# Moving the steps of a hybrid decoder layer's small work between the big products: five places in the order, and one scaling from VectorE to ScalarE

## The chip, the cores and the metric

The kernel runs on one core of a Trainium2 chip. Its time is the device time of one execution in microseconds, as the median of several runs. A core has a matrix engine (TensorE, PE in the profile), a vector engine (VectorE, DVE), a scalar engine (ScalarE, ACT), GpSimd (POOL) and a queue engine (SP) that issues transfers. Each engine takes its instructions in the order in which they were written; between engines there are semaphores.

## What is computed

One layer over 256 tokens of 2048 features, all in float32: RMS norm, one input projection into everything that four token mixers need (queries, keys, values, two kinds of gates), four attention mixers, a projection of each, a gated sum, an output projection and a final norm.

```python
h = rms_norm(x, norm_w)
p = h @ w_in                       # z, gate, qkv of four mixers, indexer, forget gate
o_dsa  = dsa_attention(...)        # 16 index heads score keys, the top 64 are kept
o_fox  = forgetting_attention(...)
o_diff = differential_attention(...)   # two softmax maps, then an RMS norm per head
o_dil  = dilated_attention(...)
for b in range(4):
    y = branches[b] * silu(z_parts[b])
    term = sigmoid(g_parts[b]) * (y @ w_branch[b])
    merged = term if merged is None else merged + term
return rms_norm(x + merged @ w_out, final_norm_w)
```

## The kernel before

**Products.** A float32 product is made of three matmuls: the weights are split into a high part (whi, ScalarE, L193) and a residue (wlo, VectorE, L206), the activations likewise, and L362, L363 and L364 multiply high by high, high by low and low by high. The work is a list of *units*, each one weight tile of 1 MB in two halves; weights arrive by SP's queue in six slots (raw), and a slot is loaded again when its last reader has been issued. whi has a ring of 8 halves, wlo a ring of 6 (HI and LO). In the main loop (L1201 ff.) each half of unit i first issues the residue five halves ahead and the high part seven halves ahead, then the matmuls of its own.

**Strassen steps.** The projections of 2048 by 1024 columns are done by `seven`: block products (c2 and c1, each in two units of 24 matmuls, and the plain P1, P2 and P4) and forms in which sums of weight blocks multiply sums of activations (P3, P5, P6, P7). `plus` (L173, tile raw) adds one weight block to another on VectorE; sf is the sum of activations, split like the others (L428 ScalarE, L429 VectorE). Units P1 to P7 have 12 matmuls and `cost` 12, the c units 24. The order of the eleven units is the list returned at the end of `seven`: one for the projections of the branches, one (`late`) for the output.

**Threads.** All small work (attention, the indexer, norms, merging) is written as Python generators. After each unit its cost is added to `since`; when it reaches PACE, 20, every active thread is advanced to its next `yield`, and only then is a unit's own `start` list made active (`begin`). So where a thread's small products stand among TensorE's big ones, and where its VectorE and ScalarE work stands in their queues, is decided by the `yield` count and by the costs. The threads that matter here:
- `rms_thread`: 1/rms of the tokens as a row (rp on TensorE, rrow), ahead of branch 0; next to it the misc thread turns the indexer's and gate's columns (msT, mtp, fl, fe, lf, then the cumulative sums cps) and the bias tables (vps).
- The index thread of branch 0: ps_ix on TensorE, rel on ScalarE, sc on VectorE (L735, L737), then four steps of top-k (L745, L746: MAX and MATCH_REPLACE).
- The attention heads: logits (lps), exponential (lg), the division by the sum (`scaled`, L795), transposes (ptp), o, the gated result y and its two halves yT. In the diff branch od, a norm (`on`), and otd, its transpose.
- `merge_thread(n)`: adds the merged gates (L908, g), turns them (mtp, L916) into mT with its residue (L921). The output's products read mT.

In the threads one ring of four PSUM tiles (`att_ps`) serves all small products.

```python
since += u.cost
if since >= PACE:
    since = 0
    run_threads()
begin(u)
```

Of the kernel before, what the change touches and what calls it, by code (L numbers as in the profile page):

```python
# [81 lines left out]
class Unit:  # L82
# [5 lines left out]
    def __init__(self, raw, mm, post=(), need=(), start=(), pre=(), frees=None, loads=None):  # L88
        self.raw, self.k0, self.nk, self.n = raw, raw.k0, raw.nk, raw.n
        self.mm, self.post = mm, list(post)  # L90
        self.need, self.start, self.pre = list(need), list(start), list(pre)
        self.after = []
        self.frees = [raw] if frees is None else list(frees)
        self.loads = [raw] if loads is None else list(loads)
        self.parts = [[None, None], [None, None]]
        self.cost = 24

    def hi(self, k):
# [11 lines left out]
def body(ctx: ExitStack, tc, x, norm_w, w_in, fox_b_f, lq1, lk1, lq2, lk2, subln_w,  # L110
# [166 lines left out]
    def rms_thread():  # L277
# [9 lines left out]
        for t in range(2):  # L287
            nc.gpsimd.tensor_scalar(dg[:, t * P:(t + 1) * P], ident, rst[:, t:t + 1], None,
                                    op0=ALU.mult)
        yield  # L290
        yield
# [140 lines left out]
    def seven(src, c1, c2, base, ev, name, need={}, start=(), late=False):  # L432
# [47 lines left out]
        def unit(what, raw, mm, post=(), frees=(), loads=(), pre=()):  # L480
# [8 lines left out]
        u3 = unit("P3", B22, product("Z", form(0, 4), not late))  # L489
        u6 = unit("P6", B12, product("Y", form(0, 0)), [read(ev.u2, "Y")],  # L490
                  pre=[lambda: plus(B12, B22), lambda: free([B22])])
        u7 = unit("P7", B11, product("Y", form(1, 0)), [read(ev.u3, "Y")], frees=[B11],
                  pre=[lambda: plus(B11, B12, ALU.subtract)])
        u2 = unit("P2", B21, product("X", whole(0, s0 + 4), True))
        u2.after += [lambda: plus(B21, B12)] + ([] if late else [lambda: free([B12])])
        u4 = unit("P4", B21, product("Y", whole(1, s0 + 4)), frees=[B21])
# [6 lines left out]
        if late:  # L503
            u6.after += [lambda: free([B12])]
            u7.post += [read(ev.c12, "Z", True), read(ev.c22, "W", True)]
            return [c2a, c2b, u1, u5, u3, u2, u6, u7, c1a, u4, c1b]
        c2b.post += [read(ev.c12, "Z", True)]
# [285 lines left out]
    def scaled(e, r):  # L793
        for t in range(2):
            nc.vector.tensor_scalar(e[:, SL[t]], e[:, SL[t]], r[:, t:t + 1], None, op0=ALU.mult)  # L795

# [38 lines left out]
    def diff_thread(b, h):  # L835
# [40 lines left out]
        yield  # L876
        yield
        ot = att_ps("otd")
        for t in range(2):
# [22 lines left out]
    def merge_thread(n):  # L902
# [6 lines left out]
        if n < 2:  # L909
            load_m(n + 2)  # L910
        yield
        for i2 in range(2):
            tp = att_ps("mtp2")
# [14 lines left out]
    def branch_units(b, n):  # L928
        def ev(ps):
# [6 lines left out]
            elif n == 0:  # L936
                for i in range(2):
                    load_m(i)
        return tok_units(w_branch[b], n * 512, lambda k: (V["yT"][:, k, 0], V["yT"][:, k, 1]),
                         (0, 2, 4, 5)[n:n + 1], ev,  # L940
                         "ps_b", need=[f"att{b}"] if n == 0 else [],
                         start=[(f"merge{n}", lambda: merge_thread(n))] if b == 3 else [])


# [140 lines left out]
    for b, off, scale, fn in ((0, O_DSA, HSCALE, head_thread), (1, O_FOX, HSCALE, head_thread),  # L1085
                              (2, O_DIFF, 0.125, diff_thread), (3, O_DIL, HSCALE, head_thread)):
        units += qkvz_units(b, off, scale, att_threads(b, fn))
        for i in range(2):
# [107 lines left out]
    for i in range(RAMP, len(units)):  # L1196
        u = units[i]
        while any(a[0] in u.need for a in active):
            run_threads(u.need)
        for h in range(2):  # L1200
            low(2 * i + h + LO - 1)  # L1201
            high(2 * i + h + HI - 1)
            u.mm(u, h)
        for f in u.post:
            f()
        since += u.cost
        if since >= PACE:
            since = 0
            run_threads()
        begin(u)  # L1210
    while active:
# [27 lines left out]
```

## Time and profile before

| | |
|---|---|
| median of 3 runs | 1010.71 us (1009.23 to 1011.93) |
| the profiled execution | 1009.36 us |
| its span in the trace | 1007.7 us |
| TensorE (PE) busy | 958.3 us, 95% |
| VectorE (DVE) busy | 856.1 us, 85% |
| ScalarE (ACT) busy | 630.1 us, 63% |
| GpSimd (POOL) busy | 47.5 us, 5% |

The span is the time from the first to the last instruction that the trace shows. Engines overlap, so their busy times don't add up. A busy share is an average over the stages: the norm and the indexer's products to about 61 us, then four branches of about 209 us each (two `seven` products for q, k, z, v, two for the gates, four branch products), then the output from about 896 us.

### The profile page before, as it was taken

The page shows a single profiled execution, that of the slowest core. Times are in us where ns is not written, and L with a number is a line of the kernel's source. Part 1 is how long each engine was busy: PE and PEld are TensorE (multiplying, and loading weights), DVE is VectorE, ACT ScalarE, POOL GpSimd, SP SyncE. Part 2 cuts the span into 40 slices and gives each one's busy share as a digit, 9 for nine tenths or more (in the row PEclk, how much of TensorE's full clock was granted, in tenths as well). Part 3 has the DMA queues.
Part 4 walks back from the last instruction along what each step waited for, and adds up shares of the span by engine and source line. Part 5 has one row for each costly group of instructions (what it writes and reads, how often), then busy time and mean ns, then how long its engine had stood idle before and what let it go on. Part 6 is the DMA issues. An engine that isn't in the chain of part 4 may idle for free.

```text
span 1007.7 us, 12090 instructions
## 1 busy us (share of the span) xinstructions
PE 958.3 (95%) x4443; PEld 793.4 (79%) x4443; DVE 856.1 (85%) x1016; ACT 630.1 (63%) x809; POOL 47.5 (5%) x67
## 2 busy tenths in 40 slices
PE   9979996999999999999999999979999999985996
PEld 8857885778888888888888877868888888873786
DVE  5689999999898989987997998968898998499762
ACT  5756853697655667974566778745556796353541
POOL 2010000000000000000100000101000000100130
PEclk9999999899999999999999999989999999987999
DMA  9926463455767556468857464648755645931702
GB/s 319 295 90 222 139 212 122 168 167 204 264 220 238 180 170 235 173 201 260 233 173 246 170 202 132 213 164 207 257 182 173 220 174 201 392 135 42 264 29 84
DMA packets 100043, 195.81 MB, mean 194 GB/s; under 512 B 7811, under 2 KB 10021, under 8 KB 99600
## 3 DMA queue, kind: packets, MB, share of 16 engines
q1 hardware_dynamic: 96240, 181.06, 52.8%
q0 software_dynamic: 3712, 13.98, 5.3%
q8 instruction: 35, 0.57, 0.2%
q14 instruction: 24, 0.20, 0.1%
q10 hardware_dynamic: 32, 0.01, 0.0%
HBM read 186.61 MB, written 8.41 MB: 194 GB/s over the span
## 4 chain that ended last, share of the span: by engine, by line
PE 81%; DVE 10%; issue 3%; ACT 3%; DMA 2%; POOL 0%; ACTq 0%; POOLq 0%; DVEq 0%
PE ps_g L362 10%; PE ps_g L363 10%; PE ps_g L364 10%; PE ps_zv L362 5%; PE ps_zv L364 5%; PE ps_zv L363 5%; PE ps_qk L364 5%; PE ps_qk L362 5%; PE ps_qk L363 5%; DVE wlo L206 4%; PE ps_o L363 2%; PE ps_b L362 2%; PE ps_b L363 2%; PE ps_b L364 2%; PE ps_o L362 2%
## 5 line engine op out<-in xcount | busy, mean ns | idle before, releaser
L193 ACT ACTIVATE whi<-raw 128x1024 fp32r<-128x1024 f32 (+1 forms) x439 | 444.6, 1051 | 231.2 <-DVE raw L173 93.3
L206 DVE TENSOR_TENSOR wlo<-raw,whi 128x1024 fp32r<-128x1024 f32 (+1 forms) x439 | 519.0, 1218 | 52.5 <-ACT whi L193 19.1
L173 DVE TENSOR_TENSOR raw<-raw 128x2048 f32<-128x2048 f32 x68 | 155.6, 2288 | 30.8 <-DMA raw<-in_w_in_dram 30.2
L364 PE MATMUL ps_g<-wlo,hT 128*128 128x512 f32 x352 | 137.7, 391 | 8.3 <-DVE wlo L206 8.3
L362 PE MATMUL ps_g<-whi,hT 128*128 128x512 f32 x352 | 138.9, 395 | 1.4 <-ACT g L530 1.4
L363 PE MATMUL ps_g<-whi,hT 128*128 128x512 f32 x352 | 137.3, 390 | 0.0
L364 PEld LDWEIGHTS ps_g<-wlo,hT 128*128 128x128 f32 x352 | 66.3, 188 | 22.7 <-DVE wlo L206 8.7
L362 PEld LDWEIGHTS ps_g<-whi,hT 128*128 128x128 f32 x352 | 66.3, 188 | 15.9 <-ACT g L530 1.8
L363 PEld LDWEIGHTS ps_g<-whi,hT 128*128 128x128 f32 x352 | 66.3, 188 | 13.4
L362 PE MATMUL ps_zv<-whi,hT 128*128 128x512 f32 x176 | 68.9, 391 | 0.0
L364 PE MATMUL ps_zv<-wlo,hT 128*128 128x512 f32 x176 | 68.6, 390 | 0.0
L363 PE MATMUL ps_qk<-whi,hT 128*128 128x512 f32 x176 | 68.5, 389 | 0.0
L363 PE MATMUL ps_zv<-whi,hT 128*128 128x512 f32 x176 | 68.5, 389 | 0.0
L362 PE MATMUL ps_qk<-whi,hT 128*128 128x512 f32 x176 | 68.5, 389 | 0.0
L364 PE MATMUL ps_qk<-wlo,hT 128*128 128x512 f32 x176 | 68.5, 389 | 0.0
L362 PE MATMUL ps_g<-whi,sf 128*128 128x512 f32 x128 | 54.2, 423 | 0.7 <-DVE tok L544 0.7
L362 PE MATMUL ps_b<-whi,yT 128*128 128x512 f32 x128 | 51.7, 404 | 0.0
L363 PE MATMUL ps_b<-whi,yT 128*128 128x512 f32 x128 | 51.2, 400 | 0.0
L364 PE MATMUL ps_b<-wlo,yT 128*128 128x512 f32 x128 | 51.1, 399 | 0.0
L363 PE MATMUL ps_g<-whi,sf 128*128 128x512 f32 x128 | 50.9, 397 | 0.0
L364 PE MATMUL ps_g<-wlo,sf 128*128 128x512 f32 x128 | 50.7, 396 | 0.0
L362 PE MATMUL ps_o<-whi,mT 128*128 128x512 f32 (+1 forms) x112 | 41.3, 369 | 0.0
(265 smaller groups left out, 1527.4 us busy)
## 6 DMA issues: line engine op xcount, KB each, us to landing
raw<-in_w_in_dram SPq DMA_DIRECT2D x132, 1024.0 KB, 5.1
raw<-in_w_branch_dram SPq DMA_DIRECT2D x16, 1024.0 KB, 5.2
raw<-in_w_out_dram SPq DMA_DIRECT2D x16, 1024.0 KB, 5.8
md<-g POOLq DMA_DIRECT2D x12, 512.0 KB, 5.3
raw<-in_w_in_dram SPq DMA_DIRECT2D x7, 512.0 KB, 9.6
xs<-in_x_dram SPq DMA_DIRECT2D x8, 256.0 KB, 8.1
mp<-md POOLq DMA_DIRECT2D x4, 512.0 KB, 3.7
xf<-in_x_dram POOLq DMA_DIRECT2D x2, 1024.0 KB, 10.9
```

What stands on the lines that cost most here:

```text
L173: nc.vector.tensor_tensor(to.tile, of.tile, to.tile, op=op)
L193: nc.scalar.activation(u.parts[0][h][:, s_], raw[:, s_], AF.Copy)
L206: nc.vector.tensor_tensor(u.parts[1][h][:, s_], raw[:, s_], u.parts[0][h][:, s_].bitcast(F32), op=ALU.subtract)
L362: nc.tensor.matmul(ps, ahi, u.hi(k)[:, cols], start=first, stop=False, skip_group_check=on)
L363: nc.tensor.matmul(ps, alo, u.hi(k)[:, cols], start=False, stop=False, skip_group_check=on)
L364: nc.tensor.matmul(ps, ahi, u.lo(k)[:, cols], start=False, stop=last, skip_group_check=on)
```

## The change

Six edits. `rms_thread` gets one more `yield`. The diff thread gets one more `yield` ahead of otd. `merge_thread(0)` gets one more `yield`, and the last unit of branch 3 makes its merge thread active before the threads are advanced, not after. All units of branch 0's first two `seven` products have cost 24, so that the threads are advanced after each. In the output's `seven` P2 moves ahead of P5, P1 and P2 cost 24, and the three weight additions that follow from the order move with it. `scaled` becomes a ScalarE activation with a scale.

```diff
@@ class Unit
         self.cost = 24
+        self.eager = False
@@ rms_thread
         yield
         yield
+        yield
         rp = att_ps("rp")
@@ seven
-        u6 = unit("P6", B12, product("Y", form(0, 0)), [read(ev.u2, "Y")],
-                  pre=[lambda: plus(B12, B22), lambda: free([B22])])
+        second = [lambda: plus(B12, B22), lambda: free([B22])]
+        fourth = [lambda: plus(B21, B12), lambda: free([B12])]
+        u6 = unit("P6", B12, product("Y", form(0, 0)), [read(ev.u2, "Y")])
...
-        u2.after += [lambda: plus(B21, B12)] + ([] if late else [lambda: free([B12])])
...
         if late:
-            u6.after += [lambda: free([B12])]
+            u5.after += second[:1]
+            u3.after += second[1:]
+            u6.after += fourth
+            u1.cost = u2.cost = 24
             u7.post += [read(ev.c12, "Z", True), read(ev.c22, "W", True)]
-            return [c2a, c2b, u1, u5, u3, u2, u6, u7, c1a, u4, c1b]
+            return [c2a, c2b, u1, u2, u5, u3, u6, u7, c1a, u4, c1b]
+        u6.pre += second
+        u2.after += fourth
@@ scaled
-            nc.vector.tensor_scalar(e[:, SL[t]], e[:, SL[t]], r[:, t:t + 1], None, op0=ALU.mult)
+            nc.scalar.activation(e[:, SL[t]], e[:, SL[t]], AF.Copy, scale=r[:, t:t + 1])
@@ diff_thread
         yield
         yield
+        yield
         ot = att_ps("otd")
@@ merge_thread
         yield
+        if n == 0:
+            yield
         for i2 in range(2):
@@ branch_units
+        units[0].eager = b == 3 and n == 3
+        return units
@@ the list of units
+        first = qkvz_units(b, off, scale, att_threads(b, fn))
+        if b == 0:
+            for u in first:
+                u.cost = 24
+        units += first
@@ main loop
+        if u.eager:
+            begin(u)
         since += u.cost
         if since >= PACE:
             since = 0
             run_threads()
-        begin(u)
+        if not u.eager:
+            begin(u)
```

The lines of the changed kernel stand up to 19 further down (L364 to L366 are L362 to L364 of before). Three places show how it moves instructions.

**TensorE at the start of branch 0.** ps_misc and ps_qk are big products (ps_qk<-whi,sf are twelve-matmul forms, ps_qk<-whi,hT plain ones). Before, the end of the misc products and the first form, u5:

```order
L372 MATMUL ps_misc<-hT,wlo 84x256
L293 MATMUL rp<-dg,ones 128x256
L362 MATMUL ps_qk<-whi,sf 128x512
L363 MATMUL ps_qk<-whi,sf 128x512
L364 MATMUL ps_qk<-wlo,sf 128x512
```

Now, the end of that form, the small products, and the first plain product, u1:

```order
L364 MATMUL ps_qk<-whi,sf 128x512
L365 MATMUL ps_qk<-whi,sf 128x512
L366 MATMUL ps_qk<-wlo,sf 128x512
L295 MATMUL rp<-dg,ones 128x256
L652 MATMUL mtp<-ident,msT 128x84 x2
L316 MATMUL vps<-oh_sb,co_sb 13x383
L364 MATMUL ps_qk<-whi,hT 128x512
```

And one form (u3) later, where c2a begins behind the last of these rows; before, cps and the first ps_ix stood behind c2a's first units:

```order
L364 MATMUL ps_qk<-whi,sf 128x512
L365 MATMUL ps_qk<-whi,sf 128x512
L366 MATMUL ps_qk<-wlo,sf 128x512
L671 MATMUL cps<-tri,lf 4x128
L672 MATMUL cps<-ones,lf 4x128
L673 MATMUL cps<-tri,lf 4x128
L674 MATMUL cps<-lf,tri 128x4
L675 MATMUL cps<-lf,ones 128x4
L676 MATMUL cps<-lf,tri 128x4
L733 MATMUL ps_ix<-ki_hi,qi 128x128
L734 MATMUL ps_ix<-ki_lo,qi 128x128
```

rp moved behind u5, mtp and vps from behind u1 to ahead of it, cps and ps_ix to ahead of c2a.

**VectorE in the second half of branch 0's first products.** Before, all four top-k steps stood in one piece behind these rows, ahead of the gates' first residues:

```order
L173 TENSOR_TENSOR raw<-raw 128x2048
L206 TENSOR_TENSOR wlo<-raw,whi 128x1024 x3
L539 SCALAR_TENSOR_TENSOR v<-ps_zv,rst,v 128x512
L737 SCALAR_TENSOR_TENSOR sc_125<-rel,wi,sc_125 128x128 x2
L737 SCALAR_TENSOR_TENSOR sc_126<-rel,wi,sc_126 128x256 x2
L206 TENSOR_TENSOR wlo<-raw,whi 128x1024 x4
L745 MAX m_1519<-sc_125 128x8
L746 MATCH_REPLACE sc_125<-m_1519,sc_125 128x128
```

Now residues and a weight addition stand between the steps, and all of it ahead of the first v:

```order
L752 MAX m_1258<-sc_126 128x8
L753 MATCH_REPLACE sc_126<-m_1258,sc_126 128x256
L207 TENSOR_TENSOR wlo<-raw,whi 128x1024
L174 TENSOR_TENSOR raw<-raw 128x2048
L207 TENSOR_TENSOR wlo<-raw,whi 128x1024
L752 MAX m_1253<-sc_125 128x8
L753 MATCH_REPLACE sc_125<-m_1253,sc_125 128x128
```

The first top-k step stood behind the third of four v rows and now stands ahead of the first; the score additions that stood at the v rows moved up too.

**TensorE between the branch products and the output's.** Before, the turns of merge 2 between the two c2 units (those of merge 0 and 1 stood one branch unit and one output unit earlier, those of merge 3 one later):

```order
L364 MATMUL ps_o<-wlo,mT 128x512
L916 MATMUL mtp_7255<-ident,g 128x128 x4
L916 MATMUL mtp_7262<-ident,g 128x128 x4
L362 MATMUL ps_o<-whi,mT 128x512
L363 MATMUL ps_o<-whi,mT 128x512
```

Now, the same place, with merges 2 and 3 together:

```order
L366 MATMUL ps_o<-wlo,mT 128x512
L926 MATMUL mtp_7256<-ident,g 128x128 x4
L926 MATMUL mtp_7263<-ident,g 128x128 x4
L926 MATMUL mtp_7270<-ident,g 128x128 x4
L926 MATMUL mtp_7277<-ident,g 128x128 x4
L364 MATMUL ps_o<-whi,mT 128x512
```

The turns of merges 0 and 1 stand likewise together, behind the last branch unit and ahead of c2a. After c2b now come P1 and P2, 24 matmuls on mT, ahead of the first that reads sf; before it was P1 alone.

## Rows read from the trace of the kernel before

**Rows 1.** Waits of TensorE: total us, times, longest us.

```profile
PE ps_o L362 <- ACT sf L428: 11.7, 1, 11.7
PE ps_g L364 <- DVE wlo L206: 8.3, 1, 8.3
PE otd L880 <- DVE on L873: 5.7, 1, 5.7
PE rp L293 <- DVE qf L399: 5.0, 1, 5.0
PE mtp L916 <- DVE g L908: 3.3, 1, 3.3
...
PE ps_g L362 <- ACT g L530: 1.4, 1, 1.4
```

**Rows 2.** Windows behind two waits; busy us per engine, granted clock, DMA share, GB/s.

```profile
176.78:185.70 8.92, 8.18 (x19) 6.04 (x20) 8.92 (x7) 6.61 (x8) 0.00 (x0) 0.50 0.29 90
...
923.70:929.80 6.10, 5.45 (x12) 3.97 (x13) 5.95 (x5) 1.95 (x2) 0.00 (x0) 0.50 0.00 0
```

**Rows 3.** Windows of 25 us in branch 0.

```profile
61.00:86.00 25.00, 19.39 (x79) 14.72 (x77) 23.59 (x30) 17.27 (x24) 0.89 (x2) 0.93 0.29 102
...
161.00:186.00 25.00, 15.97 (x55) 12.16 (x54) 24.18 (x60) 9.61 (x11) 0.00 (x0) 0.73 0.22 76
```

**Rows 4.** Timeline of VectorE, branch 0: start, us, instruction, [idle before].

```profile
72.21 0.42 DVE L399 TENSOR_TENSOR msT<-ps_misc,halves 84x256 f32<-84x256 f32 x1
...
90.54 0.17 DVE L660 SCALAR_TENSOR_TENSOR lf<-fl,fe 128x8 f32<-128x8 f32 x1 [0.71 <-ACT fe L658]
...
100.50 0.35 DVE L735 TENSOR_SCALAR sc<-rel,wi 128x256 f32<-128x256 f32 x1 [0.22 <-ACT rel L729]
...
103.06 2.29 DVE L173 TENSOR_TENSOR raw<-raw 128x2048 f32<-128x2048 f32 x1 [0.55 <-DMA raw<-in_w_in_dram]
...
150.11 2.29 DVE L173 TENSOR_TENSOR raw<-raw 128x2048 f32<-128x2048 f32 x1 [0.76 <-DMA raw<-in_w_in_dram]
...
175.51 1.22 DVE L206 TENSOR_TENSOR wlo<-raw,whi 128x1024 fp32r<-128x1024 f32 x1
...
194.79 0.55 DVE L795 TENSOR_SCALAR lg<-lg,sm 128x128 f32<-128x128 f32 x2
```

**Rows 5.** Timeline of TensorE, branch 0 and the output's start.

```profile
71.38 0.39 PE L362 MATMUL ps_qk<-whi,hT 128*128 128x512 f32 x1
...
77.95 0.39 PE L362 MATMUL ps_qk<-whi,hT 128*128 128x512 f32 x1
...
93.06 0.38 PE L664 MATMUL cps<-tri,lf 128*4 128x128 f32 x2
...
210.54 0.50 PE L362 MATMUL ps_g<-whi,hT 128*128 128x512 f32 x1 [1.41 <-ACT g L530]
...
214.76 0.27 PE L786 MATMUL ptp<-ident,lg 128*128 128x128 f32 x1
...
896.35 0.48 PE L362 MATMUL ps_o<-whi,mT 128*128 128x512 f32 x1
```

**Rows 6.** The page's transfers: KB each, us from issue to landing.

```profile
raw<-in_w_in_dram SPq DMA_DIRECT2D x132, 1024.0 KB, 5.1
```

**Rows 7.** Timeline of ScalarE, the first gates of branch 0.

```profile
201.84 1.06 ACT L193 ACTIVATE whi<-raw 128x1024 fp32r<-128x1024 f32 x1 [4.03 <-DVE raw L173]
...
214.24 0.58 ACT L593 ACTIVATE sz<-turn 128x512 f32<-128x512 f32 x1
...
216.92 0.48 ACT L790 ACTIVATE pt<-ptp 128x384 f32<-128x384 f32 x1
```

**Rows 8.** Timeline of VectorE, merge and output.

```profile
885.09 1.22 DVE L908 TENSOR_TENSOR g<-g,mp 128x1024 f32<-128x1024 f32 x1
...
903.15 1.29 DVE L921 TENSOR_TENSOR mT<-mtp,mT 128x512 fp32r<-128x512 f32 x2 [0.78 <-ACT mT L920]
...
922.73 2.36 DVE L429 TENSOR_TENSOR sf<-asum,sf 128x1024 fp32r<-128x1024 f32 x2 [1.12 <-ACT sf L428]
```

More of the change, by code (lines that the diff above doesn't have):

```diff
@@ L938, in ev @@
                     load_m(i)
-        return tok_units(w_branch[b], n * 512, lambda k: (V["yT"][:, k, 0], V["yT"][:, k, 1]),
+        units = tok_units(w_branch[b], n * 512, lambda k: (V["yT"][:, k, 0], V["yT"][:, k, 1]),
                          (0, 2, 4, 5)[n:n + 1], ev,
@@ L1086, in body @@
                               (2, O_DIFF, 0.125, diff_thread), (3, O_DIL, HSCALE, head_thread)):
-        units += qkvz_units(b, off, scale, att_threads(b, fn))
+        first = qkvz_units(b, off, scale, att_threads(b, fn))
[3 more added lines that the diff above has]
+        units += first
         for i in range(2):
```

## The prediction

> **What bounds the kernel now.** I read first what TensorE waited for [rows 1]: six waits hold most of its idle time, at 923.7, 176.8, 669.8, 66.7, 886.4 and 210.5 us. The reader is to see that five of them are the places that the change moves, and that the largest two name different things: the first a sum that ScalarE and VectorE have to form, the second one residue (wlo) of VectorE. Next the granted clock of the stretches behind the two largest [rows 2]: 0.50 in both, so 8.92 us of work behind the 8.3 us wait ran at the lower of the two levels, 1.2 GHz, and half of them, 4.46, is the price of that. Then VectorE's busy time while the first branch's products run [rows 3]: 23.59 and 24.18 of 25 us. So in that stage VectorE, not TensorE, sets the pace, though over the whole span TensorE is at 95%. The wlo that ended the second wait ran from 175.51 to 176.73 [rows 4]; TensorE went on at 176.78. In this in-order queue exactly the same VectorE instructions stand ahead of that wlo before and after; the order of them changes, the sum of their durations doesn't. Spreading the top-k burst therefore doesn't bring that wlo earlier: only idle time of VectorE between 61 and 176 us can, and there is little to take, the largest pieces being 0.76 and 0.71 [rows 4].
>
> **First branch, step by step.** *rp a step later, every unit running the threads.* The order now puts u5 (twelve products) ahead of rp, mtp and vps. TensorE does u5 instead of waiting for 5.0, but then mtp wants msT, which VectorE finishes at 72.21 + 0.42 = 72.63 [rows 4], behind nothing that has moved. The idle time stays, about 5 us, one place further on. With mtp, vps and rp about 1.3 us, u1 starts near 73.9 and not at 71.38 [rows 5]: 2.5 later.
>
> *cps and the first ps_ix ahead of c2a.* cps reads lf. Before, lf came at 90.54 [rows 4] and TensorE met it two units later, at 93.06 [rows 5], with no wait. Now cps stands between u3 and c2a. Ahead of lf VectorE has what it had before but for four wlo, each 1.22 us long with the next instruction 1.14 behind its start (175.51, [rows 4]); nor has it the wait of 0.71 for fe. So lf comes at about 90.54 - 0.71 - 4.55 = 85.3. TensorE is done with u3 at about 73.9 + 5.6 = 79.5, or 81 with part of it at the lower clock; u1, the table products and u3 took 6.57 together, 71.38 to 77.95 [rows 5]. So a new wait of about 4.5 stands ahead of cps. After cps and ps_ix (about 2.5 from 93.06 on) c2a starts at about 87.9, not at 77.95: 10 us later.
>
> *What that does to VectorE, the bound.* Behind lf it has two wlo, the small cps copies and four score adds (to about 90), then a wlo whose buffer (a ring of six) only c2a's first half frees, then the second index step's adds, whose ps_ix stands behind the whole of c2a, ending near 94 to 96 at mixed clock. VectorE idles about 4.0 in these two places (1.7 if c2a runs at full clock throughout, 4.7 if at half).
>
> *Loads.* A plus into a weight tile (raw) waits for its own transfer, 5.1 us from issue [rows 6]. Where index adds leave the stretch between the issue and the use, the wait grows: at 150.11 it was 0.76 [rows 4]; only wlo, one v and wlo (2.9) are left in between, so about 2.3, +1.5. The one at 103.06 was 0.55 and becomes about 1.1, +0.55. Gone are the waits for lf, 0.71, and for rel, 0.22 [rows 4].
>
> VectorE's net: 4.0 + 1.5 + 0.55 - 0.93 = +5.1, less the scaling of the first head that leaves it (two instructions, 194.79 to 195.26, 0.47): **+4.7** by 200 us. TensorE's later lead doesn't hide it: at 210.54 it waited 1.41 for g [rows 5], and ScalarE had stood 4.03 for raw at 201.84 [rows 7] before it could come to g. All of that comes 4.7 later. Bounds: +2.4 (idle 1.7) and +5.4 (idle 4.7).
>
> **Scaling on ScalarE.** No row shows this form on ScalarE. Below, one instruction of 384 elements takes 0.48 [rows 7]; two instructions of 256 and 128 take at most twice that, 0.96; nearest is the first with one more start, so 0.65. In the second head of the first branch ScalarE ends sz at 214.24 + 0.58 = 214.8 and would only then scale, and TensorE's ptp stood at 214.76 [rows 5]: **+0.6** (0.3 to 0.9). In the other heads the two stand further apart in the trace, so nothing there; if ScalarE were late in those eleven too, eleven times 0.6 would be 6.6. The Trainium skill ("ScalarE: Activation LUTs", "What ACT_TABLE_LOAD costs") gives 186 ns plus 0.833 per element, 93 more for a pointer operand and 93 of overlap: by an estimate from that page 0.79 for the pair, and a sum higher by 0.1; no run here shows it.
>
> **Attention's extra step.** In the order the last head's otd, the one that waits 5.7 [rows 1], still follows its od directly: the extra step moves only earlier heads' otd. Nothing: 0 (to -0.3).
>
> **Merge and output.** After the second-last branch product VectorE adds g at 885.09 [rows 8]; mtp no longer stands ahead of the last branch unit, so TensorE does that unit instead of waiting 3.3. But both first merges' transposes now come ahead of c2a, and behind 885.09 VectorE has L908 and two wlo, two g, L908, wlo, raw, wlo, two g: 1.1 + 2.3 + 1.2 + 1.1 + 1.1 + 2.2 + 1.1 + 1.2 = 11.3, so the first low mT at about 897, and c2a starts no earlier than the 896.35 of before [rows 5]. TensorE's new wait there is about 5. The sum (sf) that the forms P5, P3, P6 and P7 need has the same VectorE work ahead of it as before; mT of merges 2 and 3 wait for c2a's end, idle about 1.7 against 0.78 at 903.15 [rows 8], so sf, 922.73 on VectorE before, comes about 0.8 later. What is gained: P2 (twelve products, about 2.8) is done inside the wait, and TensorE has that less to do behind sf: 2.8 - 0.8 with a little less at the lower clock: **-2.2**. Bounds: 0 (c2a at half clock delays mT and sf by 2 more) and -3.6 (sf not later, and the clock kept for part of it).
>
> **Sum.** 4.7 + 0.6 - 2.2 = +3.1; towards the small end of the first term, which I trust least, +2.3 to +3.1. On the profiled execution's 1009.36 that gives 1012 (its span of 1007.7 and 1.66 around it); that execution lies 1.35 below the median of 1010.71, so I forecast 1010.71 + 2.5 = **1013.2**. The runs shown spread over 2.7 us, 0.27%: about 0.3%, 3.0 us, is what can be told from no change.
>
> **Rivals.**
> 1. *The wait behind the burst was TensorE's own price (other side).* If c2a's lateness finds VectorE with enough work, its new idle is 0, and the load waits are paid back; VectorE comes out even, or 0.5 early through the scaling it no longer does. Then the 8.3 us wait is met by a TensorE that is itself 5 to 10 us later, the wait shrinks to under 3, and the clock stays at 1.00: some of the 4.46 [rows 2] is kept. For it speaks that the wait is one piece; against it that 210.54 waits for ScalarE, not for TensorE. -0.5 or down to -3 there, -2.2 in the output: 1005.5 to 1009, centre 1007.7. It decides from the point where VectorE's idle between 85 and 100 us stays under 1 us. The Trainium skill ("TensorE: Matmul & The Clock Gate", "Part 1: The HAM clock gate") says that the throttled state is the default and activity releases it; that agrees with 0.50 behind both long waits [rows 2], and by it alone a wait cut into pieces costs less than one.
> 2. *The output gains nothing.* The new wait ahead of c2a is of the kind that has 0.50 behind it; c2a ends 2 later, mT and sf with it, and what P2 saved is gone. 4.7 + 0.6 + 0: 1016, and to 1018 with the upper bounds (5.4 and 0.9) and sf 1 later than before.
> 3. *Nothing arrives at the end.* VectorE's and ScalarE's waits (raw for DMA, y for o) take up each shift before the next stage, as idle time of engines off the path: 1010.7, give or take 2.
>
> **How the numbers follow.** Forecast 0.45 (1010.5 to 1015.8), rival 1 0.25, rival 2 0.20, rival 3 0.10. Faster by over 0.3%: 0.17 of rival 1, 0.03 of the forecast, 0.02 of rival 3, together 0.22. Slower by over 0.3%: 0.17 of the forecast, 0.18 of rival 2, 0.01 of rival 3, together 0.36. Within: 0.42. Range 1005.5 to 1018: rival 1's low end to rival 2's high end; what it leaves out are mishaps in all heads' scaling and a gain of both the clock and the full P2.
>
> **What would show it.** Right: waits of TensorE for msT (mtp) near 67 to 73 and for lf (cps) near 81 to 85; VectorE idle of 3 to 5 between 85 and 97; the second gate unit's wlo 3 to 6 later than 176.73; a wait for mT ahead of c2a of about 5, and the wait for sf down from 11.7 to about 7.5. Wrong: no wait at cps (then lf came earlier than I counted), the gates' first products starting no later than before, sf well ahead of 923, or otd's 5.7 gone.

## The result: 0.75% slower

The changed kernel takes 1018.8 us as the median of 3 runs (1016.8 to 1018.96), the kernel before 1010.71; the ratio is 1.0075, 95% interval [1.0046, 1.0104]. The forecast was 1013.2 with a range up to 1018.0: the direction was right and most of the new waits stand where it put them, the size was too small. The profiled execution took 1018.96 us with a span of 1017.3, 9.6 more than the one before.

TensorE's waits in the changed kernel (waits view of TensorE: total us, times, longest), against [rows 1]:

```profile
PE ps_o L364 <- ACT sf L430: 7.9, 1, 7.9
PE otd L888 <- DVE on L880: 7.1, 1, 7.1
PE ps_o L365 <- DVE mT L931: 4.9, 1, 4.9
PE ps_zv L364 <- DVE sc L757: 4.7, 1, 4.7
PE mtp L652 <- DVE msT L401: 3.9, 1, 3.9
PE cps L671 <- DVE lf L667: 3.8, 1, 3.8
PE ps_o L364 <- DVE xf L1021: 2.1, 1, 2.1
...
PE ps_g L364 <- ACT g L537: 1.5, 1, 1.5
```

Four of the five waits that the change addresses are shorter or gone: the 11.7 for sf is 7.9, the 8.3 for one residue is gone and a wait of 4.7 at 163.4 stands ahead of it, rp no longer waits, mtp of the merge neither; otd's wait is longer. (The row of the 4.7 names sc; what stood in the way there is the v that empties the product's bank and now stands behind the top-k steps: it ends on VectorE at 163.29, and cps_later's trace names v.) In their place stand new ones: for msT, lf, mT and xf, 14.7 us in all. Over all rows of this view TensorE's waits rose from 41.6 to 44.8. The larger part of the 9.6 stands in another line, the page's busy times (engine, us, share of the span, instructions):

```profile
PE 964.6 (95%) x4443; PEld 796.6 (78%) x4443; DVE 849.4 (84%) x984; ACT 641.1 (63%) x841; POOL 49.6 (5%) x67
```

The same 4443 instructions were busy for 958.3 us before, 6.3 us less; more of them now ran at the lower clock, as the windows below show. That is how much; where it is lost is read from the start of the same matmul in both timelines of TensorE:

| place | before | after | later by |
|---|---|---|---|
| branch 0's gates, the product that waits for g | 210.54 | 217.68 | 7.14 |
| branch 0's first branch product | 268.13 | 276.08 | 7.95 |
| last otd of the differential branch | 669.78 | 679.10 | 9.32 |
| branch 3's first gate product | 777.30 | 786.20 | 8.90 |
| the output's first product with sf (P5) | 923.70 | 934.15 | 10.45 |
| P7 | 939.16 | 948.77 | 9.61 |
| last matmul | 999.63 | 1009.24 | 9.61 |

Of the 9.6 us, 7.95 stand in branch 0 (7.14 of them ahead of its gates' g), about one in the differential branch, 0.7 in the output. VectorE there (timeline of VectorE, changed kernel; in brackets the idle time ahead of the instruction and who ended it):

```profile
85.61 0.15 DVE L667 SCALAR_TENSOR_TENSOR lf<-fl,fe 128x8 f32<-128x8 f32 x1
...
88.76 0.41 DVE L677 TENSOR_SCALAR ncum<-cps 4x256 f32<-4x256 f32 x1 [0.73 <-PE cps L676]
...
90.22 0.28 DVE L742 TENSOR_SCALAR sc<-rel,wi 128x128 f32<-128x128 f32 x1 [0.57 <-ACT rel L736]
...
91.39 0.35 DVE L742 TENSOR_SCALAR sc<-rel,wi 128x256 f32<-128x256 f32 x1 [0.50 <-ACT rel L736]
...
95.59 1.23 DVE L207 TENSOR_TENSOR wlo<-raw,whi 128x1024 fp32r<-128x1024 f32 x1 [2.19 <-PE ps_qk L366]
97.95 0.16 DVE L331 TENSOR_TENSOR nlam<-lsum 128x1 f32<-128x1 f32 x1 [1.14 <-ACT lsum L330]
...
99.27 1.75 DVE L744 SCALAR_TENSOR_TENSOR sc<-rel,wi,sc 128x128 f32<-128x128 f32 x4 [0.97 <-ACT rel L736]
```

The reader is to see lf at 85.61, and behind it six waits of which the kernel before had only one, of 0.22 for rel [rows 4]: 0.73 + 0.57 + 0.50 + 2.19 + 1.14 + 0.97 = 6.10 us. Five of them are for products of TensorE or for what ScalarE makes of these. The sixth, 1.14 for lsum, comes from the same place: on ScalarE lsum stands behind a whi that waited 3.05 for a product of c2a. TensorE in the same stretch, and later where the 8.92 us at half clock stood before (windows: busy us and instructions of PE, PEld, DVE, ACT, POOL, then the granted clock):

```profile
81.00:86.00 5.00, 1.19 (x6) 0.68 (x5) 5.00 (x6) 4.94 (x8) 1.97 (x3) 0.89 0.53 154
86.00:96.00 10.00, 10.00 (x35) 8.05 (x34) 5.91 (x14) 3.77 (x6) 0.54 (x1) 0.54 0.40 130
...
181.00:206.00 25.00, 25.00 (x113) 20.74 (x112) 24.90 (x29) 18.50 (x24) 0.00 (x0) 1.00 0.53 181
```

From 86 to 96 TensorE was busy all the time, at 0.54 of its clock; VectorE, which had been the bound, was busy for 5.91 of these 10 us. From 181 to 206 TensorE ran at full clock, also in the stretch that [rows 2] shows at 0.50. Behind the new wait at 163.44 the clock was lowered for a shorter time (0.80 up to 172). So TensorE had regained most of that loss, and still the gates' g came 7.14 later:

```profile
217.68 0.50 PE L364 MATMUL ps_g<-whi,hT 128*128 128x512 f32 x1 [1.52 <-ACT g L537]
```

It waits for ScalarE's g as it did at 210.54 [rows 5], by 1.52 us where it was 1.41.

In the output, VectorE and TensorE (timelines of the changed kernel):

```profile
914.75 2.48 DVE L931 TENSOR_TENSOR mT<-mtp,mT 128x512 fp32r<-128x512 f32 x4 [2.72 <-ACT mT L930]
...
933.19 2.36 DVE L431 TENSOR_TENSOR sf<-asum,sf 128x1024 fp32r<-128x1024 f32 x2 [1.12 <-ACT sf L430]
...
943.41 4.62 DVE L207 TENSOR_TENSOR wlo<-raw,whi 128x1024 fp32r<-128x1024 f32 x4
947.95 0.67 DVE L1021 TENSOR_TENSOR xf<-xf,ps_o 128x512 f32<-128x512 f32 x1
```

```profile
946.26 0.39 PE L366 MATMUL ps_o<-wlo,sf 128*128 128x512 f32 x1
948.77 0.47 PE L364 MATMUL ps_o<-whi,sf 128*128 128x512 f32 x1 [2.12 <-DVE xf L1021]
```

VectorE waits 2.72 for mT where it was 0.78 [rows 8]; sf follows at 933.19, and P7 waits 2.12 for an xf that stands on VectorE behind four residues.

### The profile page after: what moved, and what is told of

The parts are those of the page before. It is cut to its first block, busy times and chain, and to the rows that moved or that the text cites. A ratio compares the mean times of both kernels' runs of the same rounds, so it can differ in the third digit from the quotient of the medians.

```text
span 1017.3 us, 12096 instructions
## 1 busy us (share of the span) xinstructions
PE 964.6 (95%) x4443; PEld 796.6 (78%) x4443; DVE 849.4 (84%) x984; ACT 641.1 (63%) x841; POOL 49.6 (5%) x67
## 5 line engine op out<-in xcount | busy, mean ns | idle before, releaser
L364 PE MATMUL ps_g<-whi,hT 128*128 128x512 f32 x352 | 138.7, 394 | 1.5 <-ACT g L537 1.5
L366 PE MATMUL ps_g<-wlo,hT 128*128 128x512 f32 x352 | 137.1, 390 | 0.0
L364 PEld LDWEIGHTS ps_g<-whi,hT 128*128 128x128 f32 x352 | 66.1, 188 | 15.9 <-ACT g L537 2.3
L366 PEld LDWEIGHTS ps_g<-wlo,hT 128*128 128x128 f32 x352 | 66.1, 188 | 13.9
L364 PE MATMUL ps_qk<-whi,hT 128*128 128x512 f32 x176 | 70.4, 400 | 0.0
L365 PE MATMUL ps_qk<-whi,hT 128*128 128x512 f32 x176 | 70.0, 398 | 0.0
L366 PE MATMUL ps_qk<-wlo,hT 128*128 128x512 f32 x176 | 69.7, 396 | 0.0
L366 PE MATMUL ps_zv<-wlo,hT 128*128 128x512 f32 x176 | 68.7, 390 | 0.6 <-DVE wlo L207 0.6
L364 PE MATMUL ps_zv<-whi,hT 128*128 128x512 f32 x176 | 69.0, 392 | 0.0
L364 PE MATMUL ps_g<-whi,sf 128*128 128x512 f32 x128 | 53.3, 417 | 0.0
L364 PE MATMUL ps_b<-whi,yT 128*128 128x512 f32 x128 | 50.6, 395 | 1.1 <-DVE g L942 1.1
L366 PE MATMUL ps_b<-wlo,yT 128*128 128x512 f32 x128 | 50.3, 393 | 0.0
L366 PE MATMUL ps_g<-wlo,sf 128*128 128x512 f32 x128 | 49.9, 390 | 0.0
```

Of the source, the lines that this page charges most:

```text
L364: nc.tensor.matmul(ps, ahi, u.hi(k)[:, cols], start=first, stop=False, skip_group_check=on)
L365: nc.tensor.matmul(ps, alo, u.hi(k)[:, cols], start=False, stop=False, skip_group_check=on)
L366: nc.tensor.matmul(ps, ahi, u.lo(k)[:, cols], start=False, stop=last, skip_group_check=on)
```

## The experiments

All ratios are to the kernel before, run on the same chip in the same rounds, with 95% intervals. The traces are single executions: in kernels that leave branch 0 as it was, branch 0's first branch product stood between 0.24 earlier and 2.19 later than in the trace of before, and the wait for g at 210 was 1.10 in one and 2.47 in another; no run explains that difference. Shifts below 2 us are therefore read from one stage to the next inside a trace, and against the medians.

### The five parts alone

**a_first.** Only the edits of the first branch:

```diff
         yield
         yield
+        yield
         rp = att_ps("rp")
...
+        first = qkvz_units(b, off, scale, att_threads(b, fn))
+        if b == 0:
+            for u in first:
+                u.cost = 24
```

> The kernel before with only the two edits of the first branch: the extra step in rms_thread and cost 24 for branch 0's first two products. Theory (VectorE is the bound until 200 us and loses time because cps and the first index step stand ahead of c2a, which then runs at the lower clock): the first wait of TensorE for lf near 85.9 us and idle time of VectorE of about 6 us between 88 and 100 are there, ScalarE's g for the gates (before at 210.54 on TensorE) comes 7 to 7.5 later, and the whole kernel is 7 to 8 us slower. Rival (the loss comes from the scaling on ScalarE and the other edits; the first branch alone only spreads its waits): less than 3 us at 210, and 0 to 3 us slower.

Measured: 1014.83 us, ratio 1.0052 [1.0040, 1.0064]. TensorE's wait for lf is there (85.90), and VectorE's idle time behind it:

```profile
88.75 0.41 DVE L671 TENSOR_SCALAR ncum<-cps 4x256 f32<-4x256 f32 x1 [0.72 <-PE cps L670]
...
94.46 1.23 DVE L206 TENSOR_TENSOR wlo<-raw,whi 128x1024 fp32r<-128x1024 f32 x1 [1.07 <-PE ps_qk L365]
96.83 0.16 DVE L330 TENSOR_TENSOR nlam<-lsum 128x1 f32<-128x1 f32 x1 [1.15 <-ACT lsum L329]
...
98.14 1.75 DVE L738 SCALAR_TENSOR_TENSOR sc<-rel,wi,sc 128x128 f32<-128x128 f32 x4 [0.96 <-ACT rel L730]
```

With 0.57 and 0.50 at 90.21 and 91.38 these are 4.97 us; the gates' g is 6.34 and branch 0's first branch product 6.35 later than in the trace of before. The theory's waits are there, its sizes (about 6, 7 to 7.5, and 7 to 8 for the whole) were too large: 0.52% are 5.3 us. This one part is two thirds of the whole loss.

**a_scaled.** Only the scaling:

```diff
-            nc.vector.tensor_scalar(e[:, SL[t]], e[:, SL[t]], r[:, t:t + 1], None, op0=ALU.mult)
+            nc.scalar.activation(e[:, SL[t]], e[:, SL[t]], AF.Copy, scale=r[:, t:t + 1])
```

> The kernel before with only scaled moved to ScalarE. Theory: VectorE saves 0.47 us once before 200 us (gates' g at 210.54 about 0.5 earlier), TensorE waits up to 0.8 more at the second head's ptp near 215; in the differential branch VectorE waits for ScalarE's scaling, the three residues ahead of the last weight addition come 1 to 1.5 later, its load is issued later, and otd at 669.78 comes 1 to 1.5 later: in all 1 to 2 us slower. Rival (the extra step in diff_thread is what made otd later): otd moves by less than 0.6, and the whole is within 1 us of before.

Measured: 1010.94 us, ratio 1.0008 [0.9999, 1.0018]. Branch 0's end is 0.79 earlier, otd 1.17 later: 1.96 are lost in between, and otd moved as the theory has it. TensorE's wait for otd is

```profile
PE otd L880 <- DVE on L873: 7.7, 1, 7.7
```

On VectorE the scaled tile is read next, and VectorE waits for it in all four heads, 4.8 us in sum:

```profile
594.09 0.88 DVE L852 SCALAR_TENSOR_TENSOR lg<-lg,sm 128x128 f32<-128x128 f32 x2 [1.74 <-ACT lg L795]
...
609.16 0.89 DVE L852 SCALAR_TENSOR_TENSOR lg<-lg,sm 128x128 f32<-128x128 f32 x2 [2.13 <-ACT lg L795]
...
639.94 2.29 DVE L173 TENSOR_TENSOR raw<-raw 128x2048 f32<-128x2048 f32 x1
...
646.06 0.88 DVE L852 SCALAR_TENSOR_TENSOR lg<-lg,sm 128x128 f32<-128x128 f32 x2 [0.72 <-ACT lg L795]
...
663.31 2.29 DVE L173 TENSOR_TENSOR raw<-raw 128x2048 f32<-128x2048 f32 x1 [2.87 <-DMA raw<-in_w_in_dram]
```

The loss is made by the first two of these waits, not by the last, on which the theory built: ahead of the first, at 587.87, VectorE's weight addition is 0.79 earlier than before, and those at 639.94 and 663.31, ahead of the last wait and behind it, are 1.13 and 1.18 later (before: 588.66, 638.81 and 662.13). In this trace the loss did not reach the end: the output's sf stands 0.44 earlier than before and the last matmul 1.17 earlier. The time can't be told from no change.

**a_merge.** Only the merge's steps:

```diff
         yield
+        if n == 0:
+            yield
         for i2 in range(2):
...
+        units[0].eager = b == 3 and n == 3
...
+        if u.eager:
+            begin(u)
```

> The kernel before with only the merge edits: the extra step in merge_thread(0) and the last branch unit's merge made active before the threads are advanced. Theory: TensorE no longer waits 3.3 at 886, but waits about 5 for the low mT ahead of c2a's second matmul; c2a runs at the lower clock, mT of merges 2 and 3 and then sf come 1.5 later; 1 to 2 us slower. Rival (the moved turns only fill a wait): sf at 923.7 or earlier, 0 to 3 us faster.

Measured: 1012.05 us, ratio 1.0018 [1.0007, 1.0029]. The wait for the low mT ahead of c2a is there, with 2.7 shorter than expected and than in the full change; the wait for g, which the theory had gone, is still 2.0, now ahead of the turns of merges 0 and 1. VectorE's wait for the mT of merges 2 and 3 is 2.77 (at 907.31):

```profile
PE ps_o L363 <- ACT sf L429: 10.5, 1, 10.5
...
PE ps_o L364 <- DVE mT L924: 2.7, 1, 2.7
```

From branch 3's gates (1.05 later than before) to sf (926.60, 2.90 later) 1.85 were lost, and the whole is 1.8 slower: in both the theory holds.

**a_late.** Only the output's order:

```diff
-            return [c2a, c2b, u1, u5, u3, u2, u6, u7, c1a, u4, c1b]
+            return [c2a, c2b, u1, u2, u5, u3, u6, u7, c1a, u4, c1b]
```

with the additions moved and the costs of 24 as in the full change.

> The kernel before with only the output's order: P2 ahead of P5 and the weight additions moved with it. Theory (behind sf VectorE's queue of eight residues, one weight addition and three xf sets when P7 may start, not TensorE): sf stays at 923.7 within 0.5, TensorE's wait for it falls from 11.7 to about 9, P7 (939.16 before) starts 0 to 1 earlier with a wait of about 2 for xf, and the whole is 0 to 1 us faster. Rival (TensorE's work behind sf is what counts): P7 2 to 2.8 earlier, the whole 2 to 3 us faster.

Measured: 1011.26 us, ratio 1.0014 [1.0005, 1.0023], slower by 1.4. P7 stands at 939.47, 0.31 later than before, with a wait of 0.78 for xf. The rival's gain is not there. The theory is right in that P7 waits for VectorE's xf, and missed its numbers: P7 is not earlier, the whole is not faster, and sf comes at 926.24, 2.54 later. On VectorE two more residues now stand ahead of the sums:

```profile
916.75 2.35 DVE L420 TENSOR_TENSOR asum<-mT 128x1024 f32<-128x1024 f32 x2
919.01 2.35 DVE L206 TENSOR_TENSOR wlo<-raw,whi 128x1024 fp32r<-128x1024 f32 x2
921.28 0.69 DVE L423 TENSOR_TENSOR asum<-asum 128x512 f32<-128x512 f32 x1
...
925.27 2.36 DVE L429 TENSOR_TENSOR sf<-asum,sf 128x1024 fp32r<-128x1024 f32 x2 [1.12 <-ACT sf L428]
```

The two residues (2.3 us) left the stretch behind sf and entered the one ahead of it. From sf to P7 it is now 13.23 us and not 15.46, so P2's time is gained there, and what sf lost pays it back: no part of the saved 2.8 us arrives at the end. From the merge to the xf ahead of P7 VectorE has 18 residues and four weight additions in either order; only where sf stands among them differs.

**a_diff.** Only the step ahead of otd (one `yield`).

> The kernel before with only the extra step ahead of otd. Theory: the last head's otd follows its od as before, so TensorE's wait of 5.7 stays and the whole is within 1 us of before. Rival (part of otd's later start in the changed kernel comes from the extra step): otd's wait grows by 0.5 to 1.5 us and the whole with it.

Measured: 1009.49 us, ratio 0.9993 [0.9984, 1.0002]. The whole is as expected, the wait isn't: otd waited 4.3, not 5.7. Measured from branch 0's end otd came 1.41 earlier, and half of that was lost again before branch 3, behind a lower clock (0.50 from 670.5 to 676; before, 0.61 from 669.7 to 675). The rival fell too: the extra step doesn't make otd later. What made otd wait 7.1 in the full change is the scaling: 7.7 with it alone, 5.6 where only this branch is left without it (scaled_heads, below).

The five ratios add up to 0.85%, the full change measured 0.75% [0.46%, 1.04%]; so nothing has to be put down to their combination. That the sums agree doesn't mean that each part loses in the full change what it lost alone: a_late has twelve residues on VectorE between the merge and sf, the full change ten, as before.

### What makes branch 0 slow

**cps_later.** a_first, with one more step ahead of cps and of the index threads' first product:

```diff
         yield
+        yield
         cps = att_ps("cps")
...
         yield
+        yield
         sc = selb[t]
```

> The two edits of the first branch as in a_first, and one more step each ahead of cps and of the index threads' first product, so that both stand behind c2a and not ahead of it. Theory (the loss of the first branch is VectorE's idle time behind the early cps and first index step): TensorE's wait for lf near 86 is gone, VectorE's idle between 85 and 100 falls from about 5 to under 2, and the branch's end comes 3 to 4.5 us earlier than in a_first; about 1012 us, 1 to 3 above before. Rival (the loss comes from taking threads at every unit as such, by the later load waits of 2.1 and ScalarE's steps): within 1.5 us of a_first.

Measured: 1010.25 us, ratio 1.0002 [0.9994, 1.0011]. TensorE's wait for lf is gone, lf itself stays at 85.72, VectorE has no wait over 0.15 us between 80 and 100, and branch 0 ends 0.71 later than in the trace of before, not 6.35; more came back than was expected. So the loss was cps and the first index step ahead of c2a, not the taking of threads at every unit. How much of it is the order and how much the lower clock behind the wait, this run doesn't separate: it took both away. The same run shows what spreading is worth:

```profile
PE mtp L646 <- DVE msT L400: 5.3, 1, 5.3
PE ps_zv L363 <- DVE v L527: 4.2, 1, 4.2
```

The top-k steps are spread here as in the change, the wait of 8.3 at 176.78 is replaced by one of 4.2 at 153.88, and the time is that of before.

**dram_b0.** The kernel before, with B12 + B22 of branch 0's first two products as accumulating transfers on GpSimd's queue:

```diff
+        for k in range(0, of.nk, 2):
+            nc.gpsimd.dma_start(dst[:, k:k + 2], of.src[...], accum_op=ALU.add)
...
-                  pre=[lambda: plus(B12, B22), lambda: free([B22])])
+                  pre=[lambda: add(B12, B22), lambda: free([B22])])
```

> The kernel before, with one of the weight additions (B12 + B22) of branch 0's two first products done by an accumulating transfer from DRAM on GpSimd's queue, in two pieces each, and not by VectorE: 2.29 us of VectorE's work less, twice. Theory (VectorE is the bound from 61 to 200 us): the second gate unit's residue (176.73 before) and the gates' g (210.54) come 3.5 to 4.5 earlier, the whole 3 to 4.5 us faster. Rival (TensorE, or the position of the top-k burst, sets it): the wait at 176 grows by as much, and nothing moves, or the transfers land late and it is slower.

Measured: 1006.59 us, ratio 0.9973 [0.9963, 0.9983]: 2.7 us faster. The gates' g is at 208.38, 2.16 earlier, and the wait at 176 shrinks instead of growing:

```profile
PE ps_g L366 <- DVE wlo L208: 6.9, 1, 6.9
```

Of 4.58 us of VectorE's work somewhat more than half arrived; its waits for loads grew, for example to 1.79 at 147.93 where [rows 4] has 0.76. So VectorE bounds the stage, though not all of what is taken off it arrives.

**scaled_heads.** a_scaled, with the differential branch's scaling left on VectorE:

```diff
-        scaled(e0, r0)
+        for t in range(2):
+            nc.vector.tensor_scalar(e0[:, SL[t]], e0[:, SL[t]], r0[:, t:t + 1], None, op0=ALU.mult)
```

> The kernel before, with scaled on ScalarE in the head threads (branches 0, 1 and 3) and on VectorE in the differential branch. Theory: the first branch keeps its gain of about 0.6 to 0.8 and otd stays where the branch puts it, so the output's start is 0.6 to 0.8 earlier than before: 0.5 to 1 us faster. Rival (the later otd of a_scaled was variation of the load ahead of it, not the scaling): otd is 1 us or more later than the stage ahead of it, as in a_scaled.

Measured: 1009.66 us, ratio 0.9990 [0.9981, 1.0000]. otd's wait is 5.6, and otd stands 0.26 earlier than before behind branches that stand 0.15 earlier. The later otd of a_scaled was the scaling. The gain of half a us to one us that was expected is not told from none.

### The output

**dram_out.** The same accumulating transfer for the output's B12 + B22, on the kernel before.

> The kernel before, with the same weight addition of the output's product done by an accumulating transfer: 2.29 us less on VectorE, ahead of sf. Theory (VectorE is the bound from 885 to 940 us): sf (923.7) and P7 (939.16) come 1.5 to 2.2 earlier, the whole 1 to 2.2 us faster; less if the next addition into B11, which reads B12, then waits for the transfer. Rival (sf waits for TensorE's products and their turns): VectorE idles instead, and sf and the whole stay within 0.5.

Measured: 1015.07 us, ratio 1.0048 [1.0036, 1.0061]. Slower: the next addition reads B12 and waits for the transfer, and sf waits behind it on VectorE.

```profile
917.53 2.29 DVE L173 TENSOR_TENSOR raw<-raw 128x2048 f32<-128x2048 f32 x1 [4.13 <-DMA raw<-in_w_out_dram]
```

Here it replaced 2.29 us of work by 4.13 us of waiting. It doesn't tell the two theories apart.

**no_plus_before.** The kernel before, with that addition left out:

```diff
-                  pre=[lambda: plus(B12, B22), lambda: free([B22])])
+                  pre=[lambda: None if late else plus(B12, B22), lambda: free([B22])])
```

> The kernel before, with the weight addition B12 + B22 of the output's product left out (so P6 and what follows from it multiply other weights): 2.29 us less on VectorE ahead of sf and, unlike the accumulating transfer, nothing that VectorE could wait for instead. Theory (VectorE's queue sets sf): TensorE's wait for sf falls by 2 from 11.7, P7 comes 2 earlier, the whole 1.5 to 2.5 us faster. Rival (sf is set by TensorE's products and their turns): VectorE idles and nothing moves.

Measured: 1010.09 us, ratio 0.9995 [0.9985, 1.0005]. The theory falls: the wait for sf is 11.1 and not 9.7, and VectorE waits instead, for the turns of the last merge:

```profile
904.00 1.29 DVE L921 TENSOR_TENSOR mT<-mtp,mT 128x512 fp32r<-128x512 f32 x2 [0.65 <-ACT mT L920]
...
910.34 1.29 DVE L921 TENSOR_TENSOR mT<-mtp,mT 128x512 fp32r<-128x512 f32 x2 [1.64 <-ACT mT L920]
```

Ahead of sf VectorE's work is not the bound alone: the mT of merges 2 and 3 waits for TensorE to come to its turns behind a c2 unit. Taking work off VectorE there only moved the wait.

**no_plus_after.** The changed kernel, with B21 + B12 left out in the output:

```diff
-        fourth = [lambda: plus(B21, B12), lambda: free([B12])]
+        fourth = [lambda: None if late else plus(B21, B12), lambda: free([B12])]
```

> The changed kernel, with the weight addition B21 + B12 of the output's product left out (so P4 multiplies other weights): in this order it stands on VectorE between sf and the xf that frees P7's bank. Theory (behind sf VectorE's queue, not TensorE's work, sets P7's start): TensorE's wait of 2.1 for xf at 948.8 shrinks to under 0.5 and the rest of the kernel comes 1.5 to 2.2 earlier, about 1016.5 us. Rival (P7's wait is covered by another, for whi or the activations): the end moves by less than 0.5 us.

Measured: 1017.5 us, ratio 1.0064 [1.0050, 1.0079]. The wait for xf is gone, and a shorter one for whi takes its place:

```profile
947.62 0.47 PE L364 MATMUL ps_o<-whi,sf 128*128 128x512 f32 x1 [0.87 <-ACT whi L194]
```

P7 comes 1.15 earlier than in the changed kernel, with sf where it was (934.22). So VectorE's queue did set P7 there, by 1.15 us; below that whi is next. This lies between theory and rival, nearer to the theory. It rests on the traces: the interval of this ratio overlaps the full change's.

### A version that beats both

**best.** The kernel before with dram_b0's and scaled_heads' edits.

> The kernel before with dram_b0's accumulating transfers and scaled_heads' scaling on ScalarE in branches 0, 1 and 3. Theory: the gains add, 3.5 and 0.5: about 1006 us, 0.35 to 0.5 per cent under before. Rival (with VectorE relieved of 4.6 us in the first branch ScalarE's chain at 210 is next, and the scaling lengthens it): no better than dram_b0.

Measured: 1006.08 us, ratio 0.9965 [0.9954, 0.9977]: 0.35% faster than before. Of the change it holds only the scaling in three branches, and none of the moved steps; it takes work off VectorE in a stage that it bounds. Whether the scaling adds to dram_b0 can't be told from these intervals.

## Why the prediction was half right

**mtp and lf: right.** The forecast had msT at 72.63 with TensorE idle about 5, and lf at 85.3 with a wait of 4.5. Measured: 72.95 with 3.88, lf at 85.61 with 3.81. Counting what the order puts ahead of an instruction, at durations of the old trace, gave the place to 0.3 us.

**c2a's start and VectorE's idle time: the step that failed first.** Forecast: cps and ps_ix take 2.5, c2a starts at 87.9, VectorE idles 4.0 (1.7 to 4.7). Measured: cps began at 85.91 and c2a at 90.43, 4.5 later where the same products took 2.4 before (93.06 to 95.50), since everything behind the wait ran at 1.2 GHz, the small products too (0.54 from 86 to 96):

```profile
85.91 0.59 PE L671 MATMUL cps<-tri,lf 128*4 128x128 f32 x2 [3.81 <-DVE lf L667]
...
90.43 0.63 PE L364 MATMUL ps_qk<-whi,hT 128*128 128x512 f32 x1
...
95.39 0.40 PE L364 MATMUL ps_qk<-whi,hT 128*128 128x512 f32 x1
```

The forecast priced the small products at full clock and only c2a at the lower one. The idle time came to 6.10, outside its bounds; 1.80 of it (0.73 for cps, 0.57 and 0.50 for rel) is the late small products, 1.14 a wait of nlam for ScalarE that the forecast didn't have. The two places that it did have idled 2.19 and 0.97, less than 4.0. So it is luck that the sign given for it, 3 to 5 between 85 and 97, was met (0.73 + 0.57 + 0.50 + 2.19 and the start of nlam's wait, about 4.2): half of that stands elsewhere. The load waits were right in the one that counted (2.44; forecast 2.3). The term was +4.7 and measured 7.14 at the gates' g: 6.10 + 1.68 + 0.09 - 0.93 for the waits that went, less 0.47 for the scaling, is 6.47; 0.3 of the rest was there before the stage began, 0.4 is not accounted for. The second gate unit's wlo, forecast 3 to 6 later, was about 7.8 later (the weight addition behind it 184.41, before 176.65).

**Scaling: price right, place half wrong.** 0.65 was taken for the pair on ScalarE; the next instruction started 0.69 later:

```profile
221.85 0.79 ACT L802 ACTIVATE lg<-lg,sm 128x128 f32<-128x128 f32 x2
222.54 1.99 ACT L194 ACTIVATE whi<-raw 128x1024 fp32r<-128x1024 f32 x2
```

The Trainium skill ("ScalarE: Activation LUTs", "What ACT_TABLE_LOAD costs") led to an estimate of 0.79 for the pair; the row has 0.79 from the first's start to the second's end, so trace and page agree. In the second head the branch lost 0.8 (7.14 to 7.95; forecast 0.6), and 0.74 in each of a_scaled, scaled_heads and best. "Nothing there" for the other heads was wrong: the forecast asked only when TensorE would need the tile. In the differential branch it is VectorE that reads the scaled tile next, and waited 5.2 us for it in four heads.

**Attention's extra step: the time right, the wait wrong.** The forecast had 0 and an unmoved wait. The part alone changed the time by nothing that can be told, but shortened otd's wait to 4.3; in the full change otd waits 7.1 since the scaling's loss is larger. The net of both is about +1.0 by branch 3. I looked at where otd stands on TensorE, not at what moved ahead of `on` on VectorE.

**Merge and output: the second step that failed.** Right were the wait ahead of c2a (about 5; 4.87) and the one for sf (about 7.5; 7.87). VectorE's idle time for mT was 2.72 and not 1.7, sf 1.55 later than the stage before and not 0.8. What failed is the 2.8 us of P2: TensorE was ready for P7 12.50 us after it began with sf (946.65 - 934.15), before it was 14.59 (939.16 - 0.87 - 923.70), so it did save 2.1. But P7 then waited 2.12 for xf and not 0.87 for whi. Of 2.8 us, 0.84 arrived, less than sf lost: +0.7 in place of -2.2. Even the 0.84 is not told from nothing: from sf to P7 it was 14.62 us, and 14.74 to 16.17 in the traces of the kernels that keep the old order, 15.46 in that of before. The sentence "TensorE has that less to do behind sf" took TensorE's work for the stage's time; VectorE's queue between sf and xf is 12.48 us long here (935.47 to 947.95) with no gap. The forecast was right that sf has the same VectorE work ahead of it as before; it didn't ask the same of xf, which has eight residues and a weight addition between sf and itself, as before. What P2 no longer does behind sf could bring P7 forward only to that xf.

**The sum.** Forecast 3.1 on the trace, measured 9.6: 2.4 from branch 0's idle time, 0.2 from the scaling in its second head, 1.0 from the differential branch, 2.9 from the output. The bounds that the forecast gave its terms, added up, run from -1.2 to +6.3 (2.4 + 0.3 - 0.3 - 3.6 and 5.4 + 0.9), and the small end of its first term would have given +0.8, not +2.3; its 1010.5 to 1015.8 was narrower than its terms, and the 8.1 us between the medians lie outside both.

**The rivals.** Rival 1 was right that the clock comes back: TensorE ran at full clock where [rows 2] has 0.50. It was worth nothing that arrives, as the forecast said: ScalarE's g ends the stage. That a wait cut into pieces costs less clock, which the forecast drew from the Trainium skill ("TensorE: Matmul & The Clock Gate", "Part 1: The HAM clock gate"), no run bears out: in cps_later the waits of 5.3 and 4.2 are each followed by a stretch at a lowered clock (0.54 from 73 to 81, 0.73 from 153.9 to 163), and in the full change the stretch behind 3.81 us of waiting (some 9 us) is as long as the one behind the 8.3 before. That the throttled state follows idleness and activity releases it, the trace agrees with: 0.54 from 86 to 96, 1.00 later. Rival 2's result (the output gains nothing) is what happened, though by P7's wait for xf more than by c2a. Its 1016 to 1018 was nearest, with a first term that was still too small.

What stays open: how VectorE and TensorE share the stretch ahead of sf. Taking 2.29 us from VectorE gave under 0.8 there (from branch 3's gates to sf), and a_diff, which changes nothing there, came 1.0 shorter in that stretch; what taking TensorE's time would give wasn't tried.

## What to carry to other kernels

The busy share over the span named TensorE (95%), and its waits were the places of the change; the stage of the longest reordering was bound by VectorE (23.6 of 25 us), and there spreading waits brought nothing while taking 4.6 us of work off VectorE brought 2.7. Before a small product is moved ahead of a big one, work out when its input is ready on the other engine: if it isn't, the big product waits and, as here behind 3.81 us, starts at the lower clock, and the engine that bounds the stage waits for both. Before work is moved to another engine, ask who reads the result next: in the differential branch it was VectorE itself. And a saving on one engine counts up to the next instruction of that engine that waits for another: read that other's queue to there.

## What the hardware showed that was not expected

Accumulating transfers of 512 KB from DRAM into SBUF on GpSimd's queue landed 5.8 to 6.2 us after their issue (median 6.0), beside plain loads of 1024 KB in 5.1:

```profile
raw<-in_w_in_dram POOLq DMA_DIRECT2D x4, 512.0 KB, 6.0
```

Two of them one behind the other replace 2.29 us of VectorE, and were a gain in branch 0 (dram_b0) and a loss in the output (dram_out), where the next addition stood waiting for them. And the part of a stage at the lower clock was longer than the wait that it followed: 3.81 us of idle time were followed by about 9 us, 85.9 to 95.1, in which c2a's matmuls started 0.43 apart, not 0.23.
